# Seventeen gate projections as pairs in front of the mixers, with the three mixer kinds alternating, in a one-core HGRN2, mLSTM and Mamba-2 trunk

## The chip, the cores and the metric

The kernel runs on one core of one Trainium2 chip. The metric is the device time of one execution in microseconds (us). The kernel before was run three times; the median is 2498.74 us.

## The reference, cut to what matters

One layer of a trunk over 1024 frames of width 1024, in float32:

```python
h = rmsnorm(x, norm1_g)
(hg_q, hg_f, hg_i, hg_g, ml_qk, ml_v, ml_if, ml_o,
 mb_z, mb_xbc, mb_dt, gate_pre) = jnp.split(h @ w_in, split_at, axis=-1)
...
y_hg = rmsnorm(o_hg) * silu(hg_g)            # 8 HGRN2 heads, out-gate hg_g
...
y_ml = rmsnorm(h_ml) * sigmoid(ml_o)         # 4 mLSTM heads, out-gate ml_o
...
y_mb = rmsnorm(y_ssd * silu(mb_z))           # 4 Mamba-2 groups of 4 heads
...
gates = sigmoid(gate_pre)                    # 3 branches of 1024 channels
mixed = gates[0] * (y_hg @ w_br_hg) + gates[1] * (y_ml @ w_br_ml) + gates[2] * (y_mb @ w_br_mb)
x = x + mixed @ w_out
x = x + conv_gated_mlp(rmsnorm(x, norm2_g))
return rmsnorm(x, final_g)
```

The three mixers read only `h`. Their order among each other is free, and so is the moment at which an output gate or a branch gate is computed, as long as it is before its use.

## The kernel before, in words

Everything lies channels on partitions, 1024 frames along the free dimension. A float32 weight block of 128 output channels (`w_raw`) is split into a rounded part `w_hi` (ACT, L99) and the rest `w_lo` (DVE, L100), as `h` was once. A product takes three matmuls: hi by hi, hi by lo, lo by hi.

**Plain blocks.** `gemm` (L115, its matmuls at L136) makes one block of 128 channels in a PSUM tile `ps_g` of 128x1024: 8 slices of the depth, 3 products, 2 halves of the frames, 48 matmuls of 128x512. `gemm_tok` (L251, matmuls at L274) makes 256 channels with frames on partitions, in two `ps_g` tiles, by 192 matmuls of 128x256. There are two `ps_g` tiles in all (pool `pg`, L55), and four small ones, `ps_m` (L56).

**Pairs.** `pair_gemm` (L174) makes two blocks together by seven products instead of eight, after `operands` (L142) has made sums of the weight quarters on DVE: 7 products of 4 slices by 3, so 84 matmuls of 128x512 (L171) where two plain blocks take 96. It needs sums of the quarters of `h` as well, the tiles `t` that `sums` (L216) makes, 8 tiles of 128x4x512.

**Order of the program.** `first` normalises `x`, keeps the unsplit `h` in DRAM (`h_dram`), begins the first two blocks of HGRN2 head 0 and makes the values `v` of heads 0 and 1. Then come 8 HGRN2 heads (`hg_head`: blocks f, q and the output gate), with `scalars` (decays and input gates of the other two kinds, L524) after the sixth; 4 mLSTM heads (`ml_head`: blocks q and k through a convolution, L626, values by `gemm_tok`, two output-gate blocks, L638); 4 Mamba groups (`mb_group`: four blocks through convolutions, `gemm_tok` for z). Then 4 branch gates as plain blocks, the sums from a reload of `h_dram` (L1182 to L1186), 16 branch gates as 8 pairs (`gate_pairs`, L847) and 4 plain ones, each kept in `gate_dram`; then the branch products, the output projection and the feed-forward part.

An HGRN2 head computes its 128x128 attention tiles level by level: for each of six levels four DVE operations and one exponential on ACT make `z` (L460 to L464), 8 small matmuls (L468) multiply, and DVE puts the result into `hgA` (`hg_put`, L505; a masked copy, L521). Only one `hgA` exists. Then follow a diagonal part (L477, L478), the outputs (L487, L489, L491), the head's norm (L500, L502, L493), and a transposition back to channels (`out_ch`, L712) with the gate multiplied in (L718). A convolution (`conv`, L601) is one ACT operation and three DVE passes over PSUM (L609), and it holds its `ps_g` tile until the third pass.

**What sets the order.** The program is not laid out by hand: a list scheduler with a cost model orders the instructions of each engine, across heads, by readiness and priority (weights have a high one, L103). The pairs alone run in the written order on PE (`in_order`, L193). Each engine then runs its list strictly in order, waiting on semaphores. Loads go through SP's queue, stores (`keep`) through POOL's.

Of the kernel before, what the change touches and what calls it, by code (L numbers as in the profile page):

```python
# [18 lines left out]
P = 128  # L19
# [28 lines left out]
class Trunk:  # L48
# [265 lines left out]

    def first(self, hp, early):

        nc, tc, ins = self.nc, self.tc, self.ins
        self.h = [[hp.tile([P, KT, HALF], F32R, name=f"h{hf}{part}", align_bytes=ALIGN) for part in range(2)]
                  for hf in range(2)]
        with tc.tile_pool(name="n1", bufs=2, side="left", reuse_waits="tile") as pool:  # L320
            xs = [pool.tile([P, KT, HALF], F32, name="n_x") for _ in range(2)]
            tmp = lambda: pool.tile([P, HALF], F32, name="n_t", bufs=6)

            def load(hf):
                for q in range(4):
                    nc.sync.dma_start(out=xs[hf][:, 2 * q:2 * q + 2], in_=ins["xT"][hf, :, 2 * q:2 * q + 2])

            def scale(hf, rs):
                for kt in range(KT):
                    t = xs[hf][:, kt]  # L330
                    nc.vector.scalar_tensor_tensor(out=t, in0=t, scalar=self.col("norm1_g", kt),
                                                   in1=rs, op0=ALU.mult, op1=ALU.mult)
                    self.split(self.h[hf][0][:, kt], self.h[hf][1][:, kt], t, nc.gpsimd if kt % 3 == 2 else None)
                self.keep(self.h_d[hf], xs[hf])
# [11 lines left out]
            vw = [self.weight_(ins["w_v"][i], [pool.tile([P, 1024], F32R, name=n, align_bytes=ALIGN) for n in ("w_hi", "w_lo")])  # L346
                  for i in range(2)]
# [11 lines left out]
        mp = early()  # L359
        v = mp.tile([P, NC_, 256], F32, name="v")  # L360
        for i, p in enumerate(pv):
            nc.scalar.copy(out=v[:, 2 * i:2 * i + 2], in_=p)
        return mp, begun, v

# [19 lines left out]
    def hg_v(self, mp, pair):  # L384
        v = mp.tile([P, NC_, 256], F32, name="v")

        def evac(cs, ps):
# [4 lines left out]
    def hg_head(self, mp, hd, v, begun=None):  # L392
        nc = self.nc
        wb = self.ins["w_hg"]
        c3 = lambda t: t.rearrange("p (c t) -> p c t", t=P)

        ps = begun[0] if begun else self.gemm(wb[3 * hd], self.rhs_h)
        f = mp.tile([P, T], F32, name="ta")
        nc.scalar.activation(out=f, in_=ps, func=AF.Sigmoid)
        ps = begun[1] if begun else self.gemm(wb[3 * hd + 1], self.rhs_h)  # L400
# [213 lines left out]
    def ml_head(self, mp, hd):  # L614
# [108 lines left out]
    def mb_group(self, mp, g):  # L723
# [423 lines left out]
def build(tc, ins, outs, dbg=None):  # L1147
    stages = dbg or dict(hg=8, ml=4, mb=4, rest=True)
    left = dict(side="left", reuse_waits="tile")
    right = dict(side="right", reuse_waits="tile")  # L1150
    with ExitStack() as ctx:
        t = Trunk(tc, ctx, ins, outs, dbg)
        t.y_dram = [outs[f"y{i}"] for i in range(3)] if dbg else [
            t.dr.tile([KT, P, T], F32, name=f"y_dram{i}") for i in range(3)]
        t.h_d = t.dr.tile([2, P, KT, HALF], F32, name="h_dram")
        t.gate_d = t.dr.tile([24, P, T], F32, name="gate_dram")
        t.x2_d = t.dr.tile([KT, P, T], F32, name="x2_dram")
        t.act_d = t.dr.tile([22, P, T], F32, name="act_dram")
        with tc.tile_pool(name="gp", bufs=3, **right) as t.gp:
            with tc.tile_pool(name="hp", bufs=1, **right) as hp:  # L1160
                with ExitStack() as ms:
                    late = ms.enter_context(tc.tile_pool(name="late", bufs=1, **right))
                    early = lambda: Mix(ms.enter_context(tc.tile_pool(name="early", bufs=1, **right)), late)
                    mp, begun, v = t.first(hp, early)
                    t.late_consts(late)
                    t.hg_setup()
                    for hd in range(stages["hg"]):
                        if hd and hd % 2 == 0:
                            v = t.hg_v(mp, hd // 2)
                        t.hg_head(mp, hd, v, begun if hd == 0 else None)  # L1170
                        if hd == 5:
                            t.scalars(mp)
                    for hd in range(stages["ml"]):
                        t.ml_head(mp, hd)
                    for g in range(stages["mb"]):
                        t.mb_group(mp, g)
                if not stages["rest"]:
                    return
                t.gates(range(GATES))
                with tc.tile_pool(name="tp", bufs=1, **right) as tp:  # L1180
                    with tc.tile_pool(name="hx", bufs=2, **left) as hx:
                        xs = [hx.tile([P, KT, HALF], F32, name="h_x") for _ in range(2)]  # L1182
                        for ks, hf in itertools.product((slice(0, KT // 2), slice(KT // 2, KT)), range(2)):
                            t.fetch(xs[hf][:, ks], t.h_d[hf][:, ks])
                        quarter = lambda hf, k0: [[t.h[hf][part][:, k0 + k] for k in range(KT // 2)] for part in range(2)]
                        t.bs = [quarter(0, 0), quarter(0, KT // 2), quarter(1, KT // 2)] + t.sums(tp, xs)  # L1186
                    with tc.tile_pool(name="a1", bufs=1, **left) as pool:
                        t.gate_pairs(pool, range(GATES, 24 - GATES, 2))
                t.gates(range(24 - GATES, 24))
# [59 lines left out]
```

## Time and profile before

| | |
|---|---|
| median of 3 runs | 2498.74 us (2498.58 to 2500.35) |
| the profiled execution | 2498.8 us, of it 2497.0 us span |
| PE busy | 2464.3 us (99%) |
| DVE, ACT, POOL busy | 1508.2, 1005.8, 62.2 us |
| mean granted TensorE clock | 0.994 |
| HBM | 177.23 MB read, 49.38 MB written |

The profile is of one execution. Busy time of PE is the union of its matmuls. An idle time stands before the instruction that ended it, with the engine and tile that released it. A row of the trace that has several instructions gives their count after "x"; a plain float32 matmul leaves two records.

### The profile page before, as it was taken

The page shows a single profiled execution, that of the slowest core. Times are in us where ns is not written, and L with a number is a line of the kernel's source. Part 1 is how long each engine was busy: PE and PEld are TensorE (multiplying, and loading weights), DVE is VectorE, ACT ScalarE, POOL GpSimd, SP SyncE. Part 2 cuts the span into 40 slices and gives each one's busy share as a digit, 9 for nine tenths or more (in the row PEclk, how much of TensorE's full clock was granted, in tenths as well). Part 3 has the DMA queues.
Part 4 walks back from the last instruction along what each step waited for, and adds up shares of the span by engine and source line. Part 5 has one row for each costly group of instructions (what it writes and reads, how often), then busy time and mean ns, then how long its engine had stood idle before and what let it go on. Part 6 is the DMA issues. An engine that isn't in the chain of part 4 may idle for free.

```text
span 2497.0 us, 31129 instructions
## 1 busy us (share of the span) xinstructions
PE 2464.3 (99%) x12980; PEld 2116.6 (85%) x12980; DVE 1508.2 (60%) x1888; ACT 1005.8 (40%) x1233; POOL 62.2 (2%) x99
## 2 busy tenths in 40 slices
PE   8999999999999999999999999999999999999998
PEld 6898989889988898998888888888878888878886
DVE  6576767873443366756765323354687887875445
ACT  4444445553433263555444312122344544542212
POOL 2000000000000000000000000000000000000000
PEclk8999999999999999999999999999999999999999
DMA  5111010111211122122333454354412222243321
GB/s 218 35 35 51 35 51 26 62 60 43 76 60 60 61 83 76 52 93 80 141 104 109 134 168 169 95 190 134 142 55 91 78 85 85 85 160 128 109 76 68
DMA packets 64141, 228.63 MB, mean 92 GB/s; under 512 B 7400, under 2 KB 8040, under 8 KB 63232
## 3 DMA queue, kind: packets, MB, share of 16 engines
q1 hardware_dynamic: 52352, 181.54, 21.9%
q0 software_dynamic: 11648, 45.09, 4.6%
q8 instruction: 102, 1.67, 0.3%
q14 instruction: 39, 0.32, 0.0%
HBM read 177.23 MB, written 49.38 MB: 91 GB/s over the span
## 4 chain that ended last, share of the span: by engine, by line
PE 96%; DVE 2%; issue 1%; ACT 1%; DMA 0%; SPq 0%; DVEq 0%; ACTq 0%
PE ps_g L136 48%; PE ps_m L171 15%; PE ps_g L274 10%; PE ps_g L171 6%; PE ps_m L136 5%; PE ps_m L468 3%; PE ps_m L801 1%; PE ps_m L274 1%; PE ps_m L477 1%; PE ps_m L712 1%; PE ps_m L683 1%; PE ps_m L487 1%; PE ps_m L440 1%; PE ps_m L663 0%; PE ps_m L685 0%
## 5 line engine op out<-in xcount | busy, mean ns | idle before, releaser
L136 PE MATMUL ps_g<-h,w_hi 128*128 128x512 f32 x2080 | 585.4, 398 | 5.8 <-DVE h L100 3.9
L99 ACT CAST w_hi<-w_raw 128x1024 fp32r<-128x1024 f32 x209 | 218.9, 1048 | 738.9 <-PE ps_g L136 541.0
L136 PEld LDWEIGHTS ps_g<-h,w_hi 128*128 128x128 f32 x2080 | 388.2, 189 | 85.6 <-DVE h L100 4.7
L100 DVE TENSOR_TENSOR w_lo<-w_raw,w_hi 128x1024 fp32r<-128x1024 f32 x209 | 254.9, 1220 | 169.3 <-ACT w_hi L99 167.4
L136 PE MATMUL ps_g<-h,w_lo 128*128 128x512 f32 x1040 | 332.3, 395 | 0.0
L274 PE MATMUL ps_g<-w_hi,h 128*128 128x256 f32 x1408 | 261.1, 284 | 0.0
L136 PE MATMUL ps_g<-p_hi,w_hi 128*128 128x512 f32 x768 | 239.5, 390 | 2.8 <-DVE x L1005 2.2
L136 PE MATMUL ps_g<-p_lo,w_hi 128*128 128x512 f32 x768 | 239.2, 389 | 0.8 <-DVE p_lo L100 0.8
L136 PE MATMUL ps_g<-p_hi,w_lo 128*128 128x512 f32 x768 | 239.4, 389 | 0.0
L136 PEld LDWEIGHTS ps_g<-h,w_lo 128*128 128x128 f32 x1040 | 195.6, 188 | 40.3
L274 PEld LDWEIGHTS ps_g<-w_hi,h 128*128 128x128 f32 x1408 | 221.3, 192 | 0.6
L274 PE MATMUL ps_g<-w_lo,h 128*128 128x256 f32 x704 | 200.1, 284 | 0.0
L136 PEld LDWEIGHTS ps_g<-p_hi,w_hi 128*128 128x128 f32 x768 | 144.0, 188 | 34.0 <-DVE x L1005 2.6
L136 PEld LDWEIGHTS ps_g<-p_lo,w_hi 128*128 128x128 f32 x768 | 144.2, 188 | 31.2 <-DVE p_lo L100 1.1
L136 PEld LDWEIGHTS ps_g<-p_hi,w_lo 128*128 128x128 f32 x768 | 144.1, 188 | 30.2 <-DVE w_lo L100 0.3
L274 PEld LDWEIGHTS ps_g<-w_lo,h 128*128 128x128 f32 x704 | 134.9, 192 | 0.5
L171 PE MATMUL ps_m<-t,w_hi 128*128 128x512 f32 x432 | 133.0, 389 | 0.0
L1005 DVE TENSOR_TENSOR x<-ps_g,x 128x1024 f32<-128x1024 f32 x40 | 49.0, 1225 | 89.3 <-PE ps_g L136 85.6
L609 DVE SCALAR_TENSOR_TENSOR gate<-c,c_vec,gate 128x1023 f32<-128x1023 f32 x76 | 95.9, 1281 | 2.0 <-ACT gate L605 1.3
L171 PEld LDWEIGHTS ps_m<-t,w_hi 128*128 128x128 f32 x432 | 81.1, 188 | 16.8
L188 ACT COPY u<-ps_m 128x512 f32<-128x512 f32 x81 | 47.6, 588 | 117.4 <-PE ps_m L171 117.4
L171 PE MATMUL ps_m<-t,w_lo 128*128 128x512 f32 x216 | 84.1, 390 | 1.5 <-DVE w_lo L100 1.5
(317 smaller groups left out, 3913.9 us busy)
## 6 DMA issues: line engine op xcount, KB each, us to landing
w_raw<-w_up SPq DMA_DIRECT2D x44, 512.0 KB, 3.3
w_raw<-w_hg SPq DMA_DIRECT2D x24, 512.0 KB, 3.3
w_raw<-w_v SPq DMA_DIRECT2D x24, 512.0 KB, 3.3
ta<-rows SPq DMA_DIRECT2D x24, 512.0 KB, 4.3
w_raw<-w_gate SPq DMA_DIRECT2D x24, 512.0 KB, 3.5
w_raw<-w_br SPq DMA_DIRECT2D x24, 512.0 KB, 4.3
w_raw<-y_dram SPq DMA_DIRECT2D x24, 512.0 KB, 4.0
gate<-gate_dram SPq DMA_DIRECT2D x24, 512.0 KB, 4.3
```

The costliest lines, as they stand in the source:

```text
L99: self.nc.scalar.copy(out=hi, in_=src)
L100: (eng or self.nc.vector).tensor_tensor(out=lo, in0=src, in1=hi.bitcast(F32), op=ALU.subtract)
L136: self.nc.tensor.matmul(out=out, lhsT=w[:, ks], rhs=rhs(part, kt, ts), start=kt == 0 and w is hi and part == 0, stop=kt == kts - 1 and w i ...
L171: self.nc.tensor.matmul(out=out, lhsT=w[x][:, ks], rhs=b[y][k], start=start and k == i == 0, stop=stop and k == 3 and i == 2, skip_group_c ...
L188: nc.scalar.copy(out=u[-1], in_=x)
L274: self.nc.tensor.matmul(out=out, lhsT=self.h[hf][part][:, 4 * i + k, o:o + P], rhs=w[:, ks], start=start and k == 0 and w is hi and part = ...
L440: nc.tensor.matmul(out=pu[:, j], lhsT=kdT[:, c], rhs=v[:, c, vs], start=True, stop=True)
L468: nc.tensor.matmul(out=pa[0:m, c], lhsT=z[:, c * P:c * P + m], rhs=part(1)[:, c], start=True, stop=True)
L477: nc.tensor.matmul(out=pa[:, j], lhsT=c3(k)[:, c + j], rhs=qs[:, c + j], start=True, stop=True)
L487: nc.tensor.matmul(out=po[:, j], lhsT=A[:, c], rhs=v[:, c, vs], start=True, stop=c == 0)
L609: end = nc.vector.scalar_tensor_tensor(out=out[:, a:ts.stop], in0=ps[:, a - d:ts.stop - d], scalar=w(d), in1=out[:, a:ts.stop], op0=ALU.mu ...
L1005: nc.vector.tensor_tensor(out=x2[j], in0=ps, in1=x2[j], op=ALU.add)
```

## The change

`first` now begins two branch-gate blocks instead of HGRN2's, makes the sums `t` directly from the normalised `n_x` (no `h_dram`), and makes the values of two head pairs, kept in `v_dram`. A new step `projections` runs 17 pairs in the written order on PE, each block through its activation into DRAM: 4 pairs of HGRN2 output gates and 4 of mLSTM output gates into `g_dram`, 9 of branch gates (2 to 19) into `gate_dram`. The mixers' heads fetch their gates from there through SP instead of computing them. The heads then come in the order of `MIXERS` (H: HGRN2, L: mLSTM, G: Mamba), with `scalars` after the second HGRN2 head. `FIRST` is 0, so that the blocks with a convolution stay in the heads. The 4 plain gates, the sums and the 8 pairs behind the mixers are gone; the last 4 plain gates stay. The scratch `n_t` has 3 buffers instead of 6.

```diff
@@ first
-            ws = [self.weight_(ins["w_hg"][j]) for j in range(2)]
+            ws = [self.weight_(ins["w_gate"][j]) for j in range(2)]
...
+            self.bs = [quarter(0, 0), quarter(0, KT // 2), quarter(1, KT // 2)] + self.sums(tp, xs)
...
+    def projections(self, pool):
...
+        for hd in range(0, 8, 2):
+            plain.append([(ins["w_hg"][3 * h + 2], self.g_d[h], AF.Silu) for h in (hd, hd + 1)])
+        for hd in range(4):
+            b = 4 * hd
+            plain.append([(ins["w_ml"][b + 2 + j], self.g_d[8 + 2 * hd + j], AF.Sigmoid) for j in range(2)])
...
+        for b in range(2, 24 - GATES, 2):
+            plain.append([(ins["w_gate"][i], self.gate_d[i], AF.Sigmoid) for i in (b, b + 1)])
...
+        for job in self.in_order(jobs):
+            cs = [pool.tile([P, T], F32, name="c", bufs=3) for _ in job]
+            self.pair_gemm(pool, [j[0] for j in job], cs)
+            for c, (_, dst, *how) in zip(cs, job):
+                g = c
...
+                nc.scalar.activation(out=g, in_=g, func=AF.Silu if len(how) == 2 else how[0])
+                self.keep(dst, g)
@@ hg_head
-        ps = self.gemm(wb[3 * hd + 2], self.rhs_h)
         g = self.gp.tile([P, T], F32, name="gate", bufs=3)
-        nc.scalar.copy(out=g, in_=ps)
-        nc.scalar.activation(out=g, in_=g, func=AF.Silu)
+        self.fetch(g, self.g_d[hd])
@@ ml_head
-            ps = self.gemm(wb[4 * hd + 2 + j], self.rhs_h)
             g = self.gp.tile([P, T], F32, name="gate", bufs=3)
-            nc.scalar.activation(out=g, in_=ps, func=AF.Sigmoid)
+            self.fetch(g, self.g_d[8 + 2 * hd + j])
@@ build
+FIRST = 0
+MIXERS = "HHLHHGHHLHHGLGLG"
...
+                with tc.tile_pool(name="tp", bufs=1, **right) as tp:
+                    t.first(hp, tp)
+                    with tc.tile_pool(name="a1", bufs=1, **left) as pool:
+                        t.projections(pool)
...
+                    for kind in MIXERS:
+                        n = at[kind]
+                        at[kind] += 1
+                        if kind == "H":
+                            if n % 2 == 0:
+                                v = t.hg_v(mp, n // 2)
+                            t.hg_head(mp, n, v)
+                            if n == 1:
+                                t.scalars(mp)
+                        elif kind == "L":
+                            t.ml_head(mp, n)
+                        else:
+                            t.mb_group(mp, n)
-                t.gates(range(GATES))
...
-                        t.gate_pairs(pool, range(GATES, 24 - GATES, 2))
                 t.gates(range(24 - GATES, 24))
```

In the changed kernel the lines of the heads are 50 higher: the levels' matmuls are L518 (before L468), their masked copies L571 (L521), the diagonal L527 and L528 (L477, L478), the outputs L537 and L539 (L487, L489), the convolution's passes L659 (L609).

Over the whole program PE loses 108 matmuls of 128x512, DVE gains 9 operations of 128x1024 and 81 of 128x512, POOL issues 20 stores of 128x1024 more and SP 20 such loads.

**Place 1: PE inside an HGRN2 head, from its state update to its outputs.** Before, in the fourth head (`h_90` and `h_91` are the split `h`; L274 is the next head pair's `gemm_tok`, whose rows go on for 62 matmuls):

```order
L440 MATMUL ps_m<-v,kT 128x128 x7
L468 MATMUL ps_m<-z 64x64 x16
L274 MATMUL ps_g<-w_hi,h_91 128x256
L274 MATMUL ps_g<-w_hi,h_90 128x256
L274 MATMUL ps_g<-w_lo,h_90 128x256
```

In the changed kernel, in the second head:

```order
L490 MATMUL ps_m<-v,kT 128x128 x7
L518 MATMUL ps_m<-z 64x64 x16
L518 MATMUL ps_m<-z 128x64 x32
L527 MATMUL ps_m<-q,k 128x192 x8
L537 MATMUL ps_m<-v,hgA_3034 128x128 x2
```

Between the levels' matmuls no others stand now; all six levels and the diagonal follow each other.

**Place 2: DVE from the first to the third pass of the convolution of the first mLSTM head's q.** Before:

```order
L609 SCALAR_TENSOR_TENSOR q<-ps_g,c_vec,q 128x1023
L443 COPY C<-ps_m 128x128
L609 SCALAR_TENSOR_TENSOR q<-ps_g,c_vec,q 128x1022
L445 SCALAR_TENSOR_TENSOR C<-C,ta,ps_m 128x128
L509 COPY hgA_596<-ps_m 64x8x64
L460 TENSOR_TENSOR z<-b 128x32x16
L461 TENSOR_TENSOR z<-b 128x32x16
L609 SCALAR_TENSOR_TENSOR q<-ps_g,c_vec,q 128x1021
```

In the changed kernel, from the second pass on (L606 to L620 belong to `scalars`, L90 are its running sums):

```order
L659 SCALAR_TENSOR_TENSOR q<-ps_g,c_vec,q 128x1022
L100 TENSOR_TENSOR w_lo<-w_raw,w_hi 128x1024
L770 SCALAR_TENSOR_TENSOR gate<-ps_m,c_vec,gate 128x512 x2
L610 COPY z<-ta 4x128
L611 TENSOR_TENSOR z<-ta,b 4x896
L615 TENSOR_TENSOR b<-kT,ta 4x1024
L90 SCALAR_TENSOR_TENSOR z<-ones,ta 16x128 x8
L659 SCALAR_TENSOR_TENSOR q<-ps_g,c_vec,q 128x1021
```

The third pass, which gives the `ps_g` tile back, stands behind the tail of head 2 and most of `scalars`.

**Place 3: DVE between an HGRN2 head and a Mamba group.** In the changed kernel, from the last put of the fourth head to the last passes of the Mamba group's two convolutions into `ta`:

```order
L571 COPY_PREDICATED hgA_3034<-c_hmask,ps_m 128x128
L541 COPY num<-ps_m 128x512
L659 SCALAR_TENSOR_TENSOR ta<-ps_g,c_vec,ta 128x1023
L848 TENSOR_TENSOR ta<-ta,c_cmask 128x1024
L659 SCALAR_TENSOR_TENSOR ta<-ps_g,c_vec,ta 128x1023
L659 SCALAR_TENSOR_TENSOR ta<-ps_g,c_vec,ta 128x1022
L541 COPY num<-ps_m 128x512
L550 TENSOR_REDUCE r<-ta 128x8
L659 SCALAR_TENSOR_TENSOR ta<-ps_g,c_vec,ta 128x1022
L659 SCALAR_TENSOR_TENSOR ta<-ps_g,c_vec,ta 128x1021
L552 RECIPROCAL r<-r 128x8
L659 SCALAR_TENSOR_TENSOR ta<-ps_g,c_vec,ta 128x1021
```

The next instruction of PE behind the head's outputs is the group's `gemm_tok`, which needs that `ps_g` tile. Before, no Mamba group followed an HGRN2 head.

## Rows read from the trace of the kernel before

**Rows 1.** The page: span, busy times, and the chain of work that ended last, by engine

```profile
span 2497.0 us, 31129 instructions
...
PE 2464.3 (99%) x12980; PEld 2116.6 (85%) x12980; DVE 1508.2 (60%) x1888; ACT 1005.8 (40%) x1233; POOL 62.2 (2%) x99
...
PE 96%; DVE 2%; issue 1%; ACT 1%; DMA 0%; SPq 0%; DVEq 0%; ACTq 0%
```

**Rows 2.** Windows: us, busy of PE, PEld, DVE, ACT, POOL, clock, DMA share, GB/s

```profile
62.50:437.50 375.00, 374.63 (x2488) 340.06 (x2488) 255.16 (x423) 175.22 (x181) 4.58 (x7) 1.00 0.12 39
437.50:500.00 62.50, 61.18 (x335) 51.66 (x334) 52.68 (x91) 36.18 (x37) 0.54 (x1) 1.00 0.19 62
1312.50:1437.50 125.00, 125.00 (x554) 103.52 (x553) 54.77 (x63) 51.32 (x61) 7.46 (x14) 1.00 0.38 123
```

**Rows 3.** Timeline, waits of PE: start, us, engine, operation, [idle before, releaser]

```profile
417.36 1.97 PE L468 MATMUL ps_m<-z 128*128 128x64 f32 x16 [0.37 <-DVE z L464]
458.23 1.06 PE L590 MATMUL ps_m<-c_ident,kT 128*128 128x128 f32 x8 [0.79 <-DVE kT L573]
462.59 1.06 PE L590 MATMUL ps_m<-c_ident,qe 128*128 128x128 f32 x8 [0.53 <-DVE qe L582]
1263.72 0.50 PE L171 MATMUL ps_m<-t,w_lo 128*128 128x512 f32 x1 [1.53 <-DVE w_lo L100]
```

**Rows 4.** Timeline, pieces of an HGRN2 head on PE and DVE

```profile
412.31 0.72 DVE L521 COPY_PREDICATED hgA<-c_hmask,ps_m 128x512 f32<-128x512 uint8 x1 [2.90 <-PE ps_m L468]
...
417.83 0.69 DVE L464 TENSOR_TENSOR z<-z,q 128x512 f32<-128x512 f32 x1
...
422.50 2.17 PE L477 MATMUL ps_m<-q,k 128*128 128x192 f32 x12
...
428.27 0.39 PE L487 MATMUL ps_m<-v,hgA 128*128 128x128 f32 x2
...
428.49 0.39 PE L489 MATMUL ps_m<-C,qe 128*128 128x128 f32 x2
...
447.09 1.04 PE L712 MATMUL ps_m<-c_ident,num 128*128 128x128 f32 x8
```

**Rows 5.** DVE's groups in the mixers: busy, mean ns | idle before, releaser

```profile
L100 DVE TENSOR_TENSOR w_lo<-w_raw,w_hi 128x1024 fp32r<-128x1024 f32 x80 | 97.8, 1222 | 146.6 <-ACT w_hi L99 146.4
...
L460 DVE TENSOR_TENSOR z<-b 128x512 f32<-128x512 f32 x48 | 32.6, 680 | 0.3
L521 DVE COPY_PREDICATED hgA<-c_hmask,ps_m 128x512 f32<-128x512 uint8 x32 | 27.4, 858 | 38.3 <-PE ps_m L468 38.3
L718 DVE SCALAR_TENSOR_TENSOR gate<-ps_m,c_vec,gate 128x512 f32<-128x512 f32 x32 | 22.3, 743 | 11.8 <-PE ps_m L712 11.7
L90 DVE TENSOR_TENSOR_SCAN b<-ones,ta 128x128 f32<-128x128 f32 x64 | 21.8, 403 | 2.6 <-ACT ta L415 2.6
...
L445 DVE SCALAR_TENSOR_TENSOR C<-C,ta,ps_m 128x128 f32<-128x128 f32 x48 | 16.5, 344 | 1.1
L478 DVE COPY_PREDICATED hgA<-c_ident,ps_m 128x256 f32<-128x256 int32 x32 | 14.8, 462 | 10.7 <-PE ps_m L477 9.8
L521 DVE COPY_PREDICATED hgA<-c_hmask,ps_m 128x128 f32<-128x128 uint8 x32 | 14.2, 444 | 1.1
...
L491 DVE COPY num<-ps_m 128x512 f32<-128x512 f32 x16 | 11.0, 685 | 15.8 <-ACT ta L490 15.8
...
L609 DVE SCALAR_TENSOR_TENSOR q<-ps_g,c_vec,q 128x1021 f32<-128x1021 f32 x8 | 10.2, 1279 | 0.2
...
L554 DVE TENSOR_TENSOR_SCAN b<-q,k 4x1024 f32<-4x1024 f32 x1 | 2.2, 2227 | 0.0
...
L545 DVE SCALAR_TENSOR_TENSOR ta<-ta 48x1024 f32<-48x1024 f32 x1 | 1.2, 1216 | 0.3 <-ACT ta L542 0.3
```

**Rows 6.** Windows of the start, columns as in rows 2

```profile
7.62:11.78 4.16, 0.00 (x1) 0.00 (x1) 3.80 (x9) 3.24 (x7) 0.00 (x0) 1.00 1.02 405
...
24.06:28.80 4.74, 4.74 (x11) 3.77 (x12) 4.74 (x7) 1.51 (x3) 4.74 (x1) 0.50 0.98 398
```

More of the change, by code (lines that the diff above doesn't have):

```diff
@@ L345, in first @@
             begun = [(w, self.rhs_h, self.gemm_w(w, self.rhs_h, spans=HALVES[:1])) for w in ws]
[L346 to L347 removed]
+            t3 = [tp.tile([P, KT // 2, HALF], F32R, name="t", align_bytes=ALIGN, bufs=8) for _ in range(2)]
+            flat = [t.rearrange("p k t -> p (k t)") for t in t3]
+            vw = [self.weight_(ins["w_v"][i], [f[:, i * 1024:(i + 1) * 1024] for f in flat]) for i in range(2)]
             dg = self.norm_sums(tmp, lambda kt: xs[1][:, kt])
@@ L358, in first @@
                 self.tok_tile(vw, c, pv[c // 2][:, c % 2])
[L359 to L363, printed above, removed]
+            quarter = lambda hf, k0: [[self.h[hf][part][:, k0 + k] for k in range(KT // 2)] for part in range(2)]
+            self.bs = [quarter(0, 0), quarter(0, KT // 2), quarter(1, KT // 2)] + self.sums(tp, xs)
+            v = [self.gp.tile([P, T], F32, name="gate", bufs=3) for _ in range(2)]
@@ new lines, in first, with evac @@
+            for i, p in enumerate(pv):
+                nc.scalar.copy(out=v[i // 2][:, (i % 2) * HALF:(i % 2 + 1) * HALF], in_=p.rearrange("p c x -> p (c x)"))
+            for i in range(2):
+                self.keep(self.v_d[0, i], v[i])
+            for i in range(2):
+                g = self.gp.tile([P, T], F32, name="gate", bufs=3)
+                nc.scalar.activation(out=g, in_=begun[i], func=AF.Sigmoid)
+                self.keep(self.gate_d[i], g)
+            def evac(cs, ps):
+                g = self.gp.tile([P, T], F32, name="gate", bufs=3)
+                nc.scalar.copy(out=g, in_=ps.rearrange("p c x -> p (c x)"))
+                self.keep(self.v_d[1, cs.start // 4], g)
@@ new lines, in first @@
+            self.gemm_tok(ins["w_v"][2:4], evac)
+    def projections(self, pool):
+        nc, ins = self.nc, self.ins
+        plain, conv = [], []
+        for hd in range(0, 8, 2):
[3 more added lines that the diff above has]
+            plain.append([(ins["w_ml"][b + 2 + j], self.g_d[8 + 2 * hd + j], AF.Sigmoid) for j in range(2)])
+            if FIRST > 0:
+                conv.append([(ins["w_ml"][b + j], self.c_d[2 * hd + j], "ml_conv", 4 * j + hd) for j in range(2)])
+        for g in range(4 if FIRST > 1 else 0):
+            b = 4 * g
+            for js in ((2, 3), (0, 1)):
+                conv.append([(ins["w_mb"][b + j], self.c_d[8 + b + j], "mb_conv", (2 * g, 2 * g + 1, 8 + g, 12 + g)[j])
+                             for j in js])
+        for b in range(2, 24 - GATES, 2):
+            plain.append([(ins["w_gate"][i], self.gate_d[i], AF.Sigmoid) for i in (b, b + 1)])
+        jobs, at = [], 0
+        for i, p in enumerate(plain):
+            jobs.append(p)
+            if (i + 1) * len(conv) // len(plain) > at:
+                jobs.append(conv[at])
+                at += 1
+        for job in self.in_order(jobs):
[3 more added lines that the diff above has]
+                g = c
+                if len(how) == 2:
+                    g = self.gp.tile([P, T], F32, name="gate", bufs=3)
+                    self.conv(g, c, *how, 4)
+                nc.scalar.activation(out=g, in_=g, func=AF.Silu if len(how) == 2 else how[0])
+                self.keep(dst, g)
@@ L385, in hg_v @@
         v = mp.tile([P, NC_, 256], F32, name="v")
+        if pair < 2:
+            for i in range(2):
+                self.fetch(v[:, 4 * i:4 * i + 4], self.v_d[pair, i].rearrange("p (c x) -> p c x", x=256))
+            return v
         def evac(cs, ps):
@@ L1164, in build @@
-                    mp, begun, v = t.first(hp, early)
+                    mp = Mix(ms.enter_context(tc.tile_pool(name="early", bufs=1, **right)), late)
                     t.late_consts(late)
                     t.hg_setup()
[L1167 to L1178, printed above, removed]
-                t.gates(range(GATES))
[L1180 to L1187, printed above, removed]
-                        t.gate_pairs(pool, range(GATES, 24 - GATES, 2))
+                    at = dict(H=0, L=0, G=0)
```

42 lines of the change are left out of this document (19 added, 23 removed).

## The prediction

> **What bounds the kernel now.** I read the page first. PE is busy 2464.3 of 2497.0 us, and the chain that ended last is 96% PE [rows 1]: the kernel is as long as its matmuls, and 32.7 us of PE's idle time is all that better order could win. So an edit pays only by matmuls removed, and costs wherever it makes PE wait. Next the windows. In the HGRN2 heads PE is busy 374.63 of 375 us, while DVE is busy 255.16 (68%); at the border to the mLSTM heads, with `scalars` inside, DVE reaches 52.68 of 62.5 (84%) and PE falls to 61.18; in the branch gate pairs PE is busy 125.00 of 125.0 and DVE only 54.77 (44%) [rows 2]. The reader is to see that DVE has much to do in the mixers and little in the pairs, and that the plain blocks between a head's small matmuls are what keeps PE busy meanwhile.
>
> The execution that I count from took 2498.8 us, 0.06 above the median. A change under 0.2% (5.0 us) is what I call the same, about what a measurement of this kernel can tell.
>
> **What goes.** Before there are 8 pairs, now 17. Each new pair replaces 96 matmuls of 128x512 by 84: 9 by 12 is 108 matmuls less, as the order of PE shows. In the pair stretch 554 such matmuls take 125.00 us, 0.2256 us each [rows 2]. 108 by 0.2256 is **-24.4 us**, all on the path. With the sums made at the start, PE's wait of 1.53 us for `w_lo` at the first pair goes; 0.37, 0.79 and 0.53 us of waits in a head and in `scalars` belong to stretches that are laid out anew [rows 3]. Together **-3.2**. Without anything new the time would be 2498.8 - 27.6 = **2471.2**.
>
> **What is added at nothing.** The 9 further pairs bring DVE 9 operations of 128x1024 at 1.22 and 81 of 128x512 at about 0.69, 67 us, into a stretch where it is busy 44% [rows 2, 5]: 17 pairs of 19 us have 180 us of DVE time free. If that cover were gone, it would show as waits for `w_lo` like the 1.53. The 20 stores and 20 loads of 0.5 MB more are set against a DMA share of 0.12 in the heads and 0.38 in the pairs. A gate's load waits on SP for its buffer, with weights queued behind it, but four `w_raw` lie ahead, some 43 us of blocks at 48 by 0.2256 each. The sums of `h` at the start run on DVE beside the 192 matmuls of the second `gemm_tok`, at least 21 us at half of 0.2256. Three scratch buffers instead of six in the norm: 0 to 3 us, since PE idles there anyway; I take 0.
>
> **What is late next.** The mixers lose 16 plain blocks of 48 matmuls (8 in HGRN2 heads, 8 in mLSTM heads), 10.8 us of cover each, but keep all DVE work. I looked through the new orders for stretches of this kind: a matmul on which DVE waits, then a run of DVE instructions, then a matmul that waits for the last of them. What DVE needs there, less what PE has to do, PE waits. DVE is priced from its groups [rows 5], in two ways. High: row means. Low: 0.08 less per instruction, since in a dense stretch nine starts from 412.31 to 417.83 are 0.61 apart [rows 4], 0.07 under the 0.680 of L460. PE is priced by 0.2256 for 128x512, 0.22 for a 128x64 or 128x128 (428.27 to 428.49), 12 records, so 6 matmuls, of the diagonal in 2.17 us with its tail (0.33 each), and 8 transposes in some 0.9 [rows 4].
>
> - Second HGRN2 head, the levels (place 1): 16 `z` operations (10.9), 5 state updates at 0.344, 2 masked copies at 0.858, 3 small copies (1.5): 26 in 15.9 us, low 13.8. PE has only the 32 level matmuls, at most 7.2. Wait 8.7, low 6.6.
> - From that head's last level to the `gemm_tok` of the first mLSTM head, whose `ps_g` comes free with the third pass of q's convolution (place 2). DVE: the rest of the head, 16 instructions (0.858, 4 by 0.462, 4 by 0.444, 2 by 0.685, 2 by 0.743, three more of 1.21, 1.22 and 0.2: 10.0); 27 of `scalars` (16 scans of 128 columns at 0.4, the long scan 2.227, ten mostly at 1.21: 18.4); 3 passes at 1.279; one `w_lo`: 47 in 33.4, low 29.7. PE: 8 by 0.33, 15 by 0.22, a block 10.8, 8 transposes: 17.7. Wait 15.7, low 12.0.
> - Third HGRN2 head, between levels: 11 in 8.4, against 23 matmuls, 5.2: 3.2, low 2.3. From its last level to the block that waits for a convolution of the first Mamba group: 40 in 28.1 against 20.1: 8.0, low 4.8.
> - Fourth HGRN2 head to the first Mamba group's `gemm_tok` (place 3): 18, of them 5 passes of 1.279, in 14.7 against 6.0: 8.7, low 7.2.
> - Eighth head to the second group, the same border: 12 in 12.3 against 3.4: 8.9, low 7.9.
>
> The sum is **+53.2, low 40.8**, over 154 DVE instructions. To the low value come hand-overs between engines and the clock. The clock: PE idled 4.16 us at the start, and the dense 4.74 us that followed it, to 28.80, ran at a granted 0.50 [rows 6], 1.2 instead of 2.4 GHz, 2.4 us lost. Five of the waits are longer than that idle time; 5 by 2.4 is 12, and 40.8 + 12 is 52.8. Both ways give 53, which I take. That is 2471.2 + 53 = **2524 us**; the low sum alone gives 2512.
>
> On the clock the Trainium skill, page "TensorE: Matmul & The Clock Gate", section "HAM oscillation — how this bites in real kernels", has a rule against such a layout: when waits between groups of matmuls are long, each group starts cold, at half the clock, every time. By that rule, added to the high sum, the time would be 53.2 and 12 above 2471.2, 2536. The trace agrees in its one case, the 0.50 behind the idle 4.16 us [rows 6]; no row of the mixers shows a wait that long.
>
> **Rivals.**
>
> - *The waits do not come (faster).* One mechanism: at the borders and levels DVE is quicker than its row means say, because those include time for PSUM and semaphores that overlaps when it runs without a break. For it: the 0.61 against 0.68. Against it: to end faster by over 5 us, the new waits must stay under 22.6, and (53.2 - 22.6) / 154 means 0.20 less per instruction, not 0.08. Where it holds fully, 2471. Chance 0.12.
> - *Half the waits.* Other idle time of DVE before a stretch, or a weight that comes early, takes one or two borders away: 53 halved is 2498, up to 2507. Nothing in the orders shows it. Chance 0.10.
> - *The clock falls in each long wait and stays low through the short matmuls behind it*, so that the levels and outputs, not only the next block, run at 1.2 GHz. The high sum and 12, and some 5 to 10 more for these: 2536 to 2546. For it: rows 6. Against it: the waits are 8 us among stretches at full clock. Chance 0.16.
> - *Weights come late* behind the gate loads in SP's queue, 16 loads that each cost a wait like the 1.53: 25 us more, 2549. The DMA share of 0.19 at the busiest mixers [rows 2] speaks against it. Chance 0.04.
>
> That the change does not do what it says is excluded by the order: the matmuls are gone, the pairs are there.
>
> **How the numbers follow.** The forecast, waits of 41 to 60 us with their clock, has 0.58: 2512 to 2532. The time is 2524. The range takes in the clock rival above and the low sum, less 6 us for prices of DVE that no row shows, below: 2506 to 2546. Faster by over 0.2%: the first rival and a little of the second, 0.14. Same: the rest of half the waits, 0.05. Slower: 0.81.
>
> **What would show it.** In the profile after: PE's busy time down by about 24 us where the clock is full, and its idle time up from 33 to 80 or more; between the pairs and the last 4 gates, waits of PE at L518, L274 and L136 with DVE (`z`, or a pass of L659) as the releaser, of 7 to 16 us, six of them and the longest at the first mLSTM head; a DVE that is 90% busy there; a granted clock of 0.5 behind the longest. The pairs at the front should show 0.2256 us per matmul with no waits. The prediction is wrong if PE stays at 99%, if the waits name SP or DMA, or if the pairs at the front wait for their operands.

## The result and the profile after

The changed kernel takes **2543.82 us** (median of 4 runs, 2540.18 to 2545.41) against 2498.66; the ratio is 1.0177, with an interval of 1.016 to 1.0195. It is 45 us slower, on the forecast side and inside the range, but 20 us beyond the forecast of 2524.

The page of the changed kernel, the lines that answer to [rows 1], with the clock of the 40 slices:

```profile
span 2542.5 us, 31185 instructions
...
PE 2462.0 (97%) x12872; PEld 2116.3 (83%) x12872; DVE 1574.1 (62%) x1978; ACT 1022.4 (40%) x1270; POOL 72.4 (3%) x117
...
PEclk8999999979989999999999999999999999999999
...
PE 94%; DVE 4%; ACT 1%; issue 1%; DMA 0%; SPq 0%; DVEq 0%; ACTq 0%
```

Read two numbers together. PE's idle time, span less busy, rose from 32.7 to 80.5, by 47.8 us. PE's busy time fell by only 2.3, from 2464.3 to 2462.0, although 108 matmuls are gone, 24.4 us of them. So the matmuls that are left take 22.1 us longer: 2498.8 - 24.4 + 47.8 + 22.1 = 2544.3, the profiled execution. The 22.1 is only a remainder here and needs a second source. The slices with an 8 or 7 in the clock row, behind the first, say where to look for it.

First the waits. PE's waits in the changed kernel (engine, line, releaser, us in total, times, longest), those of the mixers:

```profile
PE ps_g L274 <- DVE r L552: 18.0, 2, 9.0
PE ps_g L274 <- DVE q L659: 12.8, 1, 12.8
PE ps_m L518 <- DVE z L514: 7.2, 4, 5.0
PE ps_m L764 <- DVE num L543: 7.0, 2, 3.5
...
PE ps_g L136 <- ACT ta L451: 3.0, 2, 1.7
...
PE ps_m L518 <- ACT z L512: 1.6, 1, 1.6
```

These are the places that the orders named. The longest stands at the first mLSTM head; in the timeline the three passes over q that hold its `ps_g` stand far apart on DVE, with the tail of the second HGRN2 head and `scalars` between them, and PE starts when the third ends:

```profile
548.16 1.25 DVE L659 SCALAR_TENSOR_TENSOR q<-ps_g,c_vec,q 128x1023 f32<-128x1023 f32 x1
...
554.44 1.28 DVE L659 SCALAR_TENSOR_TENSOR q<-ps_g,c_vec,q 128x1022 f32<-128x1022 f32 x1
...
560.46 3.55 DVE L90 TENSOR_TENSOR_SCAN z<-ones,ta 16x128 f32<-16x128 f32 x8
564.04 1.28 DVE L659 SCALAR_TENSOR_TENSOR q<-ps_g,c_vec,q 128x1021 f32<-128x1021 f32 x1
```

```profile
551.52 1.12 PE L764 MATMUL ps_m<-c_ident,num 128*128 128x128 f32 x8 [3.52 <-DVE num L543]
565.47 0.55 PE L274 MATMUL ps_g<-w_hi,h 128*128 128x256 f32 x1 [12.83 <-DVE q L659]
```

At the borders to the Mamba groups (745 and 1109 us) the same `gemm_tok` waits 9.02 us each time. The view names `r`, but the reciprocal is only DVE's next instruction: the passes over the first `ta` end at 754.39, and PE starts at 754.54, 0.15 us behind, as at the first mLSTM head (565.32 and 565.47).

```profile
751.93 2.46 DVE L659 SCALAR_TENSOR_TENSOR ta<-ps_g,c_vec,ta 128x1022 f32<-128x1022 f32 x2
754.31 0.19 DVE L552 RECIPROCAL r<-r 128x8 f32<-128x8 f32 x1
```

```profile
754.54 0.55 PE L274 MATMUL ps_g<-w_hi,h 128*128 128x256 f32 x1 [9.02 <-DVE r L552]
```

Then the clock. Windows cut where the granted clock changes (columns as in [rows 2]); of the six in the mixers at half clock, the one from 702.59 to 706 is left out here:

```profile
511.45:531.93 20.48, 18.66 (x78) 18.35 (x79) 12.22 (x22) 2.11 (x2) 0.00 (x0) 0.50 0.00 1
...
552.41:569.47 17.06, 4.23 (x21) 4.03 (x20) 16.64 (x23) 7.46 (x8) 0.53 (x1) 0.50 0.46 162
...
675.28:682.11 6.83, 6.83 (x28) 6.83 (x27) 3.24 (x6) 0.00 (x0) 0.00 (x0) 0.50 0.16 62
...
750.38:760.62 10.24, 6.08 (x28) 6.11 (x29) 7.54 (x8) 7.50 (x12) 0.00 (x0) 0.50 0.16 54
...
1112.19:1122.43 10.24, 3.67 (x17) 3.70 (x18) 9.95 (x10) 7.61 (x14) 0.00 (x0) 0.50 0.16 52
```

With the one left out (3.37 us busy), PE worked 42.8 us in them, at 1.2 instead of 2.4 GHz: half of it, 21.4 us, is what the clock cost, which is nearly all of the 22.1. (A further fall of 3.4 us near 2290 us, in the feed-forward part, costs some 1.7; at the start the half clock covers less work than before, which about makes up for it.) The most costly window is not behind the longest wait. It is the second HGRN2 head's levels, where 18.66 of 20.48 us are busy: after a wait of 5.05 us the short matmuls, with waits of 1.16 and 0.65 between them, all ran at half clock:

```profile
511.42 7.04 PE L518 MATMUL ps_m<-z 128*128 128x64 f32 x32 [5.05 <-DVE z L514]
519.62 3.65 PE L518 MATMUL ps_m<-z 128*128 128x64 f32 x16 [1.16 <-DVE z L514]
523.92 3.65 PE L518 MATMUL ps_m<-z 128*128 128x64 f32 x16 [0.65 <-DVE z L514]
527.37 5.06 PE L527 MATMUL ps_m<-q,k 128*128 128x192 f32 x16
```

The pairs in front did as forecast: from 62.5 to 437.5 us, which is the end of `first`, the pairs (to 422 us) and the first plain blocks of the heads, PE is busy 375.00 of 375 at full clock, with DVE at 186.62 (50%).

```profile
62.50:437.50 375.00, 375.00 (x1781) 315.93 (x1779) 186.62 (x235) 163.68 (x198) 21.69 (x40) 1.00 0.35 117
```

### The profile page after: what moved, and what is told of

It reads as the page before. It is cut to its first block, busy times and chain, and to the rows that moved or that the text cites. A ratio compares the mean times of both kernels' runs of the same rounds, so it can differ in the third digit from the quotient of the medians.

```text
span 2542.5 us, 31185 instructions
## 1 busy us (share of the span) xinstructions
PE 2462.0 (97%) x12872; PEld 2116.3 (83%) x12872; DVE 1574.1 (62%) x1978; ACT 1022.4 (40%) x1270; POOL 72.4 (3%) x117
## 4 chain that ended last, share of the span: by engine, by line
PE 94%; DVE 4%; ACT 1%; issue 1%; DMA 0%; SPq 0%; DVEq 0%; ACTq 0%
PE ps_g L136 40%; PE ps_m L171 19%; PE ps_g L274 10%; PE ps_g L171 8%; PE ps_m L136 5%; PE ps_m L518 3%; PE ps_m L856 1%; PE ps_m L527 1%; PE ps_m L274 1%; PE ps_m L764 1%; PE ps_m L735 1%; PE ps_m L715 0%; PE ps_m L737 0%; PE ps_m L840 0%; PE ps_m L827 0%
## 5 line engine op out<-in xcount | busy, mean ns | idle before, releaser
L136 PE MATMUL ps_g<-h,w_hi 128*128 128x512 f32 x1504 | 425.4, 398 | 9.9 <-DVE h L100 3.9
L136 PEld LDWEIGHTS ps_g<-h,w_hi 128*128 128x128 f32 x1504 | 280.5, 189 | 69.0 <-DVE h L100 4.7
L274 PE MATMUL ps_g<-w_hi,h 128*128 128x256 f32 x1408 | 268.4, 290 | 30.9 <-DVE r L552 18.0
L274 PEld LDWEIGHTS ps_g<-w_hi,h 128*128 128x128 f32 x1408 | 226.3, 196 | 32.1 <-issue 18.4
L136 PE MATMUL ps_g<-h,w_lo 128*128 128x512 f32 x752 | 240.2, 395 | 0.0
L274 PE MATMUL ps_g<-w_lo,h 128*128 128x256 f32 x704 | 203.2, 289 | 0.0
L171 PE MATMUL ps_m<-t,w_hi 128*128 128x512 f32 x576 | 177.3, 389 | 0.0
L136 PEld LDWEIGHTS ps_g<-h,w_lo 128*128 128x128 f32 x752 | 141.4, 188 | 29.3
L274 PEld LDWEIGHTS ps_g<-w_lo,h 128*128 128x128 f32 x704 | 137.9, 196 | 0.4
L171 PEld LDWEIGHTS ps_m<-t,w_hi 128*128 128x128 f32 x576 | 108.1, 188 | 22.4
L188 ACT COPY u<-ps_m 128x512 f32<-128x512 f32 x108 | 63.4, 587 | 156.5 <-PE ps_m L171 156.5
L183 DVE TENSOR_TENSOR c<-ps_g,u 128x512 f32<-128x512 f32 x72 | 49.7, 690 | 123.6 <-PE ps_g L171 123.6
L171 PE MATMUL ps_m<-t,w_lo 128*128 128x512 f32 x288 | 112.0, 389 | 0.0
```

The costliest lines, as they stand in the source:

```text
L136: self.nc.tensor.matmul(out=out, lhsT=w[:, ks], rhs=rhs(part, kt, ts), start=kt == 0 and w is hi and part == 0, stop=kt == kts - 1 and w i ...
L171: self.nc.tensor.matmul(out=out, lhsT=w[x][:, ks], rhs=b[y][k], start=start and k == i == 0, stop=stop and k == 3 and i == 2, skip_group_c ...
L183: add = lambda out, p, q: nc.vector.tensor_tensor(out=out, in0=p, in1=q, op=ALU.add)
L188: nc.scalar.copy(out=u[-1], in_=x)
L274: self.nc.tensor.matmul(out=out, lhsT=self.h[hf][part][:, 4 * i + k, o:o + P], rhs=w[:, ks], start=start and k == 0 and w is hi and part = ...
```

## The experiments

Two causes were mixed in the change: the output gates leave the heads (less cover), and the mixers alternate (new borders). And two costs: idle time and clock. The place of `scalars` goes with the order: behind the second HGRN2 head in the change's order, behind the sixth where all eight HGRN2 heads come first. The scheduler lays out the whole program anew for every edit, so more than the edited lines can move. Ratios are against the kernel before, with 95% intervals.

**Order of before, 17 pairs.** Edit:

```diff
-MIXERS = "HHLHHGHHLHHGLGLG"
+MIXERS = "HHHHHHHHLLLLGGGG"
...
-                            if n == 1:
+                            if n == 5:
                                 t.scalars(mp)
```

> The changed kernel with its 17 pairs in front, but the mixers in the order of before (8 HGRN2, 4 mLSTM, 4 Mamba; scalars after the sixth HGRN2 head). Theory A (the output gates taken out of the heads leave the levels without cover): the waits stay, 40 us or more, the clock falls, 2520 to 2545. Theory B (the alternation makes the long waits: a convolution holds its ps_g tile behind an HGRN2 head's tail and scalars): no wait over 4 us; the same counting as in the prediction gives 12 us (low) in levels, no fall of the clock; 2498.7 - 24.4 - 1.5 + 12 to 16 = 2485 to 2489.

Measured 2517.22 us, 1.0071 (1.0056 to 1.0086): between the two. No wait in the mixers is longer than 3.3 us, as theory B said, but there are 18 of them, and for over half of their time ACT, not DVE, is the releaser:

```profile
PE ps_m L518 <- DVE z L514: 7.0, 3, 3.3
PE ps_g L136 <- ACT ta L451: 6.3, 4, 2.5
...
PE ps_m L482 <- DVE ta L475: 2.9, 2, 1.4
```

My counting followed DVE alone and found 12 us. And the clock fell behind waits that short, in five stretches between 524 and 836 us, against theory B: PE's busy time is 2462.5, again over 22 us more than what the matmuls come to. The mean clock there:

```profile
480.00:840.00 360.00, 334.46 (x2118) 301.31 (x2117) 274.25 (x465) 165.46 (x171) 5.09 (x8) 0.95 0.13 45
```

**Alternation alone.** The 8 HGRN2 and 8 mLSTM output gates are plain blocks in their heads again, only the 9 branch-gate pairs stand in front; `MIXERS` as in the change.

```diff
+        ps = self.gemm(wb[3 * hd + 2], self.rhs_h)
...
-        self.fetch(g, self.g_d[hd])
+        nc.scalar.copy(out=g, in_=ps)
+        nc.scalar.activation(out=g, in_=g, func=AF.Silu)
...
+            ps = self.gemm(wb[4 * hd + 2 + j], self.rhs_h)
...
-            self.fetch(g, self.g_d[8 + 2 * hd + j])
+            nc.scalar.activation(out=g, in_=ps, func=AF.Sigmoid)
```

> The alternating order, but the output gates as plain blocks in their heads again; only the 9 branch-gate pairs stand in front. One pair more than before: -2.7, and the wait of 1.5 goes. Theory A (missing cover): no new waits, 2494 to 2496. Theory B (the alternation): the long wait at the first mLSTM head's gemm_tok stays, 12.5 (low) to 16 us, and 5 us in levels; with a half clock behind the long one (2 to 8 us) 2514 to 2524. The borders to the Mamba groups show no wait of 9 us in either.

Measured 2529.42 us, 1.0117 (1.0102 to 1.0132), some 5 us over theory B's range. The long wait at the first mLSTM head is there with all cover in place, and those at the Mamba borders are not:

```profile
PE ps_g L274 <- DVE q L658: 12.1, 1, 12.1
...
PE ps_g L136 <- ACT q L453: 3.9, 1, 3.9
...
PE ps_m L764 <- DVE num L542: 3.5, 1, 3.5
PE ps_m L517 <- DVE z L513: 3.3, 1, 3.3
```

**Only the front.** The same with the mixers in the order of before, 9 pairs in front.

```diff
-MIXERS = "HHLHHGHHLHHGLGLG"
+MIXERS = "HHHHHHHHLLLLGGGG"
...
-                            if n == 1:
+                            if n == 5:
                                 t.scalars(mp)
```

> The kernel of the second experiment (output gates plain in their heads, 9 branch-gate pairs in front) with the mixers in the order of before: what is left of the change is the move to the front by itself. One pair more than before, -2.7, and the wait at the first pair goes, -1.5; waits of 1 and 3 us for ACT in the HGRN2 heads as in the third experiment, with a little half clock: 2494 to 2500. If the front (sums out of the first norm, values of two head pairs by DRAM, three scratch buffers) costs something, 2502 or more; then the third experiment's 2490 would hide it.

Measured 2501.63 us, 1.0011 (1.0002 to 1.0021), between the two ranges. The waits of 1 and 3 us are there. ACT's own timeline shows where the longer one comes from, with PE's next matmul below:

```profile
428.38 1.05 ACT L99 CAST w_hi<-w_raw 128x1024 fp32r<-128x1024 f32 x1 [8.17 <-PE ps_g L136]
429.44 1.28 ACT L453 ACT_TABLE_LOAD   x1
430.74 1.02 ACT L453 ACTIVATE q<-ps_g 128x1024 f32<-128x1024 f32 x1
```

```profile
431.81 1.26 PE L136 MATMUL ps_g<-h,w_hi 128*128 128x512 f32 x4 [3.01 <-ACT q L453]
```

The `Silu` of q, which gives a `ps_g` tile back, stands in ACT's list behind the rounding of a weight block. ACT sits idle for 8.17 us until PE lets it round, then rounds, loads a table of activation functions for 1.28 us and only then does the `Silu`. The three together take 3.4 us, for 3.01 of which PE has nothing to do. Before the other wait, of 1.00, a table load of the same length stands too. In the profiled execution (2499.2 us, the fastest of ten) these two waits, 4.0 us, are most of the 4.6 by which it misses the forecast gain of 4.2; the nine others took 1.5 to 3.9 us more, at a mean clock of 0.992 to 0.994 against its 0.995. So what the front gains it loses again in the heads behind it.

This completes a square. With the 8 output-gate pairs' matmuls (96 by 0.2256 = 21.7) taken off, the corner without waits is 2501.6 - 21.7 = 2479.9. Alternation alone costs 2529.4 - 2501.6 = 27.8. Taking the gates out, in the order of before, costs 2517.2 - 2479.9 = 37.3. Both together cost 2543.8 - 2479.9 = 63.9, about their sum (65.1): **two causes of like size**, neither of which explains the result alone. "Alternation" here takes in the earlier place of `scalars`.

**HGRN2 gates back, mLSTM gates in pairs.** Order of before, 13 pairs.

```diff
-        for hd in range(0, 8, 2):
-            plain.append([(ins["w_hg"][3 * h + 2], self.g_d[h], AF.Silu) for h in (hd, hd + 1)])
```

> Order of before, HGRN2 gates plain in the heads, mLSTM gates and branch gates as 13 pairs in front. Both theories: cover in the HGRN2 heads as before, 5 pairs more than before, 60 matmuls by 0.2256 = -13.5, and -1.5 for the wait at the first pair: 2483 to 2485, no wait over 2 us in the mixers, clock 0.99. If pairs in front cost something of their own (stores, sums at the start), it shows here as the difference.

Measured 2490.32 us, 0.9966 (0.9953 to 0.9979), 5 us over the forecast: the waits of 1.0 and 3.0 us for ACT are here as well. Against the kernel with 9 pairs this is -11.3 for 4 pairs, whose matmuls come to 10.8: in this order the mLSTM heads give up their gates for nothing. It is the HGRN2 heads that cannot: the kernel with their gates in pairs as well is 26.9 slower, where its matmuls are 10.8 less, so those gates cost 37.7.

**Copies that free PSUM early.** The changed kernel, with ACT copying each block out of `ps_g` before the passes:

```diff
-            self.conv(t, ps, "mb_conv", blk, 4)
+            self.conv(t, self.out_of_psum(ps), "mb_conv", blk, 4)
...
+    def out_of_psum(self, ps):
+        raw = self.gp.tile([P, T], F32, name="gate", bufs=3)
+        self.nc.scalar.copy(out=raw, in_=ps)
+        return raw
```

(and likewise for the mLSTM blocks).

> The changed kernel, but in every convolution ACT first copies the block from PSUM to a gate buffer and the passes read that, so that a ps_g tile is free after one ACT operation instead of three DVE passes. 24 ACT copies of about 1 us more, on an engine that is 40% busy. Theory: the three longest waits (12.83, 9.02, 9.02) were for ps_g tiles held by the passes: they go, with the half clock behind them (13.98 us of work at half clock, 7 us): 2543.8 - 31 - 7 and some 5 to 10 of new waits for ACT, 2510 to 2516; the levels' waits of 6.9 us stay. Rival: DVE as a whole is too slow there, and the waits move to the next instruction that needs DVE: 2535 to 2550.

Measured 2508.93 us, 1.0036 (1.0023 to 1.0049): 34.9 less than the changed kernel, with the same matmuls, and just under the first range. All three long waits at `gemm_tok` are gone, and the waits in the second head's levels too, which I expected to stay; ACT is late in their place:

```profile
PE ps_g L136 <- ACT ta L451: 8.9, 2, 7.9
PE ps_g L136 <- ACT q L456: 6.8, 3, 3.4
PE ps_m L769 <- DVE num L543: 4.0, 2, 3.5
```

DVE is as busy as in the changed kernel (1573.9 and 1574.1 us), so the rival, DVE's whole load, did not hold: the long waits were for PSUM tiles that DVE's passes held, as the 0.15 us between pass and matmul says too. In the profile 24.8 us of the gain are PE's idle time and 10.4 its busy time, with the same matmuls. The order of the heads' levels moved too, so not all of the 34.9 is the copies' own.

**`scalars` earlier.** The changed kernel with this edit:

```diff
-                            if n == 1:
+                            if n == 0:
                                 t.scalars(mp)
```

> The changed kernel with scalars after the first HGRN2 head instead of the second. If its 27 DVE instructions behind the second head make that border the worst, the 12.83 falls to about 9, as at the two Mamba borders, and the levels' waits of 5.05, 1.16 and 0.65 with the half clock from 511 to 532 go, since the head's levels are laid out between other blocks; some waits of 1 to 2 us come at the new place: 2543.8 - 10 - 10, 2520 to 2528. If the border waits for the convolution alone, whatever stands around it, 2538 to 2545.

Measured 2528.01 us, 1.0116 (1.0101 to 1.0131), at the upper end of the first range: 15.8 us less than the changed kernel, by this edit alone. The wait at the first mLSTM head fell to about what the Mamba borders have:

```profile
PE ps_g L274 <- DVE r L552: 18.0, 2, 9.0
PE ps_g L274 <- DVE q L659: 8.5, 1, 8.5
```

**Filling the waits.** The changed kernel with 26 useless matmuls in the second head's levels; what they write is overwritten by the level's own.

```diff
+            if hd == 1:
+                self.fill(pa.rearrange("p c t -> p (c t)"), (0, 0, 20, 0, 4, 2)[li])
...
+    def fill(self, out, n):
+        for _ in range(n):
+            self.nc.tensor.matmul(out=out, lhsT=self.h[0][0][:, 0, 0:P], rhs=self.h[0][0][:, 0, :], start=True, stop=True)
```

> The changed kernel with 26 matmuls of 128x512 added whose results are overwritten: in the second HGRN2 head 20 ahead of the third level's, 4 and 2 ahead of the fifth's and sixth's, where PE waits 5.05, 1.16 and 0.65 us for DVE; 5.9 us of PE work more. If a good part of the loss there is the clock (in the changed kernel 0.50 from 511 to 532 us, with 18.66 us of PE's work in it, so 9.3 us lost), the added work keeps it up and the kernel gets faster by 5 to 9 us: 2535 to 2539. If only the idle time counts: 2543 to 2546; if the added work is not covered, 2550.

Measured 2537.62 us (2534.42 to 2539.18; the changed kernel had 2540.18 to 2545.41), 1.015 (1.0133 to 1.0167), in the first range. 5.9 us of work were added and the kernel became 6.2 us faster. The stretch of the levels, first in the changed kernel, then in this one (windows, columns as in [rows 2]):

```profile
500.00:536.00 36.00, 28.92 (x170) 27.70 (x168) 24.33 (x45) 8.15 (x10) 1.64 (x3) 0.72 0.15 53
```

```profile
500.00:530.00 30.00, 27.93 (x208) 24.86 (x206) 24.49 (x47) 7.95 (x10) 1.49 (x2) 1.00 0.19 70
```

The clock stays at 1.00, DVE does the same 24 us of work, and the stretch is 6 us shorter. The third and fourth level's matmuls, which took 7.04 us at half clock, take 3.76. But the scheduler also laid out the levels anew around the added matmuls: the last two levels, which start 4.30 us apart in the changed kernel (519.62 and 523.92), now follow each other directly:

```profile
512.76 3.76 PE L520 MATMUL ps_m<-z 128*128 128x64 f32 x32 [0.28 <-DVE z L514]
519.81 3.76 PE L520 MATMUL ps_m<-z 128*128 128x64 f32 x32 [0.56 <-DVE z L514]
```

So a good part of the loss there was clock, as the short matmuls' own times show; how the 6 us divide between the clock and the new order is not shown.

**Other blocks in the 17 pairs.** All output gates plain in their heads; in front the 16 convolution blocks of the Mamba groups (with their passes) and 18 branch gates; `scalars` after the sixth head. The new constants name the heads and groups whose blocks go in front:

```diff
-FIRST = 0
-MIXERS = "HHLHHGHHLHHGLGLG"
+MIXERS = "HHHHHHHHGLGLGLGL"
+HG_FRONT = ()
+ML_GATES = ()
+ML_CONVS = ()
+MB_CONVS = ((0, 0), (1, 0), (2, 0), (3, 0), (0, 1), (1, 1), (2, 1), (3, 1))
```

> Again 17 pairs in front, so the same 108 matmuls less, but other blocks: the 16 convolution blocks of the Mamba groups (with their DVE passes) as 8 pairs and the 9 branch-gate pairs; all output gates stay plain in their heads; HGRN2 heads first, then Mamba groups and mLSTM heads in turn. If what decides is which block leaves which stretch: -24.4 and -1.5, against them waits as in the third experiment (1.0 and 3.0 in the HGRN2 heads, ACT) and about 1 us at each of three borders: 2498.7 - 25.9 + 8, so 2479 to 2485, clock 0.99. If pairs in front with a trip through DRAM cost something of themselves, it stays at 2495 or more.

Measured 2480.35 us, 0.9925 (0.9911 to 0.994), inside the first range. The same number of matmuls as in the changed kernel, 63 us less; the order of the mixers differs as well, so this is not the blocks alone. Against the kernel with 9 pairs it is -21.3 for 8 pairs, whose matmuls come to 21.7. The page, for the two numbers that the account began with:

```profile
span 2478.9 us, 31187 instructions
...
PE 2443.0 (99%) x12872; PEld 2097.7 (85%) x12872; DVE 1567.3 (63%) x1978; ACT 1056.3 (43%) x1299; POOL 72.4 (3%) x117
```

Idle 35.9, busy 21.3 below before: here most of the 24.4 arrive.

**25 pairs.** These and all other convolution blocks and the mLSTM gates; HGRN2 gates plain, the same order.

```diff
-FIRST = 0
-MIXERS = "HHLHHGHHLHHGLGLG"
+FIRST = 2
+MIXERS = "HHHHHHHHGLGLGLGL"
```

> HGRN2 gates plain in the heads; 25 pairs in front (mLSTM gates, all blocks with a convolution, branch gates); the HGRN2 heads first, then Mamba groups and mLSTM heads in turn. 17 pairs more than before: 204 matmuls by 0.2256 = -46.0, and -1.5. No convolution holds a ps_g tile in the mixers; the counting gives 2 us of waits. Theory B: 2451 to 2456. If missing cover decides by itself, the mLSTM heads and Mamba groups, which lose 32 plain blocks, show waits of DVE, 2465 and more.

Measured 2500.74 us, 1.0006 (0.9997 to 1.0016): some 45 us over theory B's range; the other one, missing cover, came true. The mLSTM heads now have no plain block, and PE waits at each one's end for its normalisation, a chain that goes between DVE and ACT (squares, sum, root, reciprocal, product), which counting DVE alone did not see:

```profile
PE ps_m L764 <- DVE num L753: 21.8, 4, 7.1
PE ps_g L136 <- DVE p_lo L100: 4.2, 4, 2.4
PE ps_m L794 <- ACT b L795: 4.0, 3, 1.5
```

Idle time is 68.6, 35.9 over before; PE's busy time is 32.1 below before instead of 46.0, so 13.9 went to the clock. Together they use up what the pairs save.

**19 pairs.** The kernel with other blocks in its 17 pairs, and the first two mLSTM heads' convolution blocks added:

```diff
-ML_CONVS = ()
+ML_CONVS = (0, 1)
```

> The kernel before this one with the convolution blocks of the first two mLSTM heads in front too: 19 pairs, 24 matmuls less than it, -5.4; two of the mLSTM heads keep only the gates' two plain blocks as cover. If that is cover enough: 2474 to 2481. If not, a wait of 3 to 7 us behind the head's normalisation, as in the kernel with 25 pairs, in two heads, with half clock behind it: 2484 to 2492.

Measured **2474.06 us** (2469.24 to 2474.53), 0.9895 (0.9881 to 0.991): 24 us faster than before and 70 faster than the change. Cover was enough, as the first range has it; the longest wait behind the start is the 3.0 for ACT in an HGRN2 head.

```profile
span 2472.8 us, 31204 instructions
...
PE 2437.3 (99%) x12848; PEld 2093.8 (85%) x12848; DVE 1582.2 (64%) x1998; ACT 1064.1 (43%) x1311; POOL 74.5 (3%) x121
```

## Why the prediction was right, and where it was short

- *Matmuls, -24.4.* Right: 0.2256 us each at full clock, and busy time shows them wherever the clock is full, as with the other 17 pairs (-21.3).
- *Waits that go, -3.2, and what was put at nothing.* Right at the pairs, where no wait is left (before, 1.53 [rows 3]). But the kernel with only the front is 2.9 us slower than before, not 4.2 faster; two waits for ACT of 1 and 3 us in its heads, which no step of mine had, are 4.0 of these 7.1.
- *The six stretches.* Right in place, and in size as a sum; single ones are off by up to 1.7 us upward and 2.8 downward. Forecast 53.2, low 40.8; measured, stretch by stretch: levels of the second head 6.9 (8.7, low 6.6); to the first mLSTM `gemm_tok` 1.0 + 3.5 + 12.8 = 17.4 (15.7, low 12.0); levels of the third head 2.0 (3.2, low 2.3); to the Mamba convolution 1.2 + 3.5 + 0.5 = 5.2 (8.0, low 4.8); the two borders 9.0 each (8.7 and 8.9). With 1.7 for ACT at 626 us that I did not count, 51.2; less the 3.2 that went, 48.0, against 47.8 in the page. In three stretches the low price is the nearer one. In the other three the wait is even above the high one; at the border behind the fourth head the run of DVE has gaps of 0.35, 0.41 and 1.07 us, for ACT and PE. The sign that I gave, six waits of 7 to 16 us, came only in part: three are that long, and the other stretches have theirs in pieces of 0.4 to 5.1 us.
- *The clock: the step that failed.* I took "5 by 2.4 is 12" and set it in place of the difference between low and high, so that in the sum of 53 there was in effect nothing for it beside the full waits. It measured 21.4, on top of 51.2. The term was mis-sized in three ways. I misread the one fall that I had: the 4.74 us do not follow the idle 4.16 directly. Between them the clock is at 0.50 as well, with 5.16 us of work in that window:

```profile
11.78:24.06 12.28, 5.16 (x12) 2.78 (x12) 11.61 (x21) 11.80 (x20) 2.20 (x3) 0.50 0.85 341
```

Half of 5.16 + 4.74 is 4.95 us lost, twice the 2.4 that I took; 5 by 4.95 is 25, close to what was measured, though with other parts: behind a wait come short matmuls with further waits, and one window lasted 20.5 us and cost 9.3. And I counted only waits longer than 4.16: the clock also fell behind waits of 0.4 to 3.5 us (675 and 703 us here, and five times in the kernel with the order of before). With 21.4 in its place the sum is 2471.2 + 51.2 + 21.4 = 2543.8. This was my third rival, "2536 to 2546", to which I gave 0.16. That the measured time lies inside my range is owed to this rival, which set the upper end.

- *The rule of the Trainium skill*, "TensorE: Matmul & The Clock Gate", section "HAM oscillation — how this bites in real kernels", was the better guide: it counts the clock on top of the full waits, which gave 2536. The trace agrees for the four longest waits, behind which the matmuls begin at half clock (behind the 12.83, two of `w_hi` take 0.63 us, against 0.40 after 569.59). The rule is about long waits; that the clock fell behind waits of 0.4 to 3.5 us as well is what the runs here add.
- *The other rivals* fell. The 0.20 us less per DVE instruction that the first needed did not come; the waits are at the forecast's price, not half of it; and no wait of PE in the mixers names SP or a DMA, so the weights did not come late.
- *My reason was half of the cause.* I put the waits down to the 16 plain blocks taken out, and in the order of before it was the 8 of the HGRN2 heads alone that cost. The square shows that alternation by itself costs 27.8 with all blocks in place; my stretches were right because they came from the new order, which holds both.

What stays open: how the 34.9 us of the copies and the 6 us of the filling divide between their cause and the moved order, and why the clock stayed low for 20.5 us in the second head's levels.

## What to carry to other kernels

Before moving dense matmuls into a cheaper place, ask of each stretch they leave what its DVE and ACT have to do meanwhile: here the HGRN2 heads paid 37 us for giving up 8 blocks of 10.8 us, the mLSTM gates and the Mamba convolutions nothing, as long as other plain blocks stayed in the mLSTM heads. Here a vector pass that held a PSUM tile, queued behind another stage's tail, cost the longest waits; giving the tile back with one copy, or keeping the stages apart, avoided them. And price a wait of PE among short matmuls by its idle time and the half clock behind it, here 51 and 21 us.

## What the runs showed of the hardware

The granted clock fell to 0.50 behind a wait of 5.05 us and stayed there for 20.48 us, of which PE was busy 18.66, with short matmuls (128x64 and 128x192) and two small waits; I had priced a fall by 4.74 us of work. Behind the waits of 12.83 and 9.02 us, where the matmuls of `gemm_tok` follow without a wait, it was back at 1.00 sooner, as the windows show. It also fell at 675.28 us, behind waits of 1.62 and 0.37 us. And useless work can pay: with 5.9 us of it, and the order that came with it, the kernel was 6.2 us faster.
